# Norm sums as columns of tokens, in a two-layer decoder trunk

## The chip, the cores and the metric

The kernel runs on one core of one Trainium2 chip. The time is the device time of one execution in microseconds. All arithmetic is float32, or float32r: numbers are split into a high and a low part, and three float32r products stand for one float32 product.

## The reference

A trunk of two layers over 1024 tokens with 1024 features. Layer 0 is an mLSTM mixer and an MLP; layer 1 is latent attention with a shared key and value path and an MLP. What matters here are the norms over features, which stand ahead of and behind every mixer and MLP, and on three latents:

```python
def rmsnorm(x, g):
    xf = x.astype(jnp.float32)
    y = xf * lax.rsqrt(jnp.mean(xf * xf, axis=-1, keepdims=True) + EPS)
    return (y * g.astype(jnp.float32)).astype(x.dtype)

x = x + g1[:, None, :] * rmsnorm(y, norm_g[l, 1])        # after a mixer
h = modulate(rmsnorm(x, norm_g[l, 2]), sh2, sc2)         # ahead of the MLP
y = sqrelu_mlp(h, mlp_w1[l], mlp_w2[l])
x = x + g2[:, None, :] * rmsnorm(y, norm_g[l, 3])
# in mla_shared_kv and mla_mixer: rmsnorm of h's input, of c_kv (256 wide) and of cq (384 wide)
```

## The kernel before

Activations stand with features on the 128 partitions and tokens along the free axis: a block is 128 features by 512 tokens, and eight blocks make one half of the tokens. The two halves are worked on as two streams that overlap. While the one half goes through the dense products of an MLP, the other half's norms, residuals, latent projections and attention are put between them.

A norm over features is then a sum over partitions and over blocks. `square_to` (L501) squares each block on ACT and adds the squares on DVE (L507) into one 128x512 tile. `sums_rstd` (L509) gets the sum over partitions with one float32 product, whose stationary operand is a 128x128 matrix of ones (L511): every partition then holds the sums of all 512 tokens. What follows runs on 128x512 tiles: mean plus EPS on DVE (L513), and `rsqrt_` (L474), which is Ln and Exp on ACT (L476, L477) and one Newton step of three DVE instructions (L478, L479, L480). The result, `rstd`, is a 128x512 tile that later instructions multiply with. `rstd_steps` (L493) does both as a generator: squares, a pause, then the sums and the chain. Only PE's products move a number across partitions here.

There are 16 such sums in the program, called below by their number in order of time: 1 and 2 (first half) and 3 and 4 (second half) belong to layer 0's `residual` (L964) and `post` (L2776); 5 to the first half's `residual` in `to_x` (L2880); 6, 7 and 8 to its `latent` (L1694: the norm of the input, of c_kv, of cq); 9 and 10 to `post_second` (L2834); 11 to the second half's `to_x`; 12, 13 and 14 to its `latent`; 15 and 16 to its `post`.

`two_streams` (L2924) sets the order on PE from there on. The generator `other` yields numbers; each number is how many steps of the dense generator are put on PE before `other` goes on. The code adds the number to what is due, takes 1 (or 0.5 for a step that is part of a group) for each dense step, and stops when nothing is due; a 0 clears what is due. Every step's PE instructions are tied behind the step before. A dense step is mostly 12 or 24 products of 128x512. On each engine the instructions run in the order in which the scheduler put them; `tc.high_priority` moves an instruction ahead in that order.

Other lines that are spoken of: L299 to L301 are the three float32r products of `mm3`; L255 is the DVE evacuation of an MLP product; L246 and L247 split weights; L520 and L521 split an activation; L549 is `along_tokens`, which spreads a 128x4 tile along tokens with four products, and L2475 makes columns of sums with four products, both at the program's start; L1722 and L1723 are the products of the third latent projection.

Of the kernel before, what the change touches and what calls it, by code (L numbers as in the profile page):

```python
# [14 lines left out]
ALU = mybir.AluOpType  # L15
AX = mybir.AxisListType

P = 128
# [64 lines left out]
def kernel(  # L83
# [54 lines left out]
    def tmc(dt=F32):  # L138
        return sb.tile([P, 512], dt, tag="tmc", bufs=TMC, name=f"tmc_{next(uid)}")
# [4 lines left out]
    def small(n, dt=F32):  # L144
        return sb.tile([P, n], dt, tag=f"sm{n}", bufs=6, name=f"sm_{next(uid)}")
# [4 lines left out]
    def pc():  # L150
        return pp.tile([P, 512], F32, tag="pc", bufs=2, name=f"pc_{next(uid)}")
# [322 lines left out]
    def rsqrt_(y, v, t):  # L474

        nc.scalar.activation(t, v, AF.Ln)  # L476
        nc.scalar.activation(y, t, AF.Exp, scale=-0.5)  # L477
        nc.vector.tensor_mul(t, y, y)  # L478
        nc.vector.scalar_tensor_tensor(t, t, -0.5, v, ALU.mult, ALU.mult)  # L479
        nc.vector.scalar_tensor_tensor(y, t, 1.5, y, ALU.add, ALU.mult)  # L480

    def last_of(g):

        while True:
            try:
                next(g)
            except StopIteration as e:
                return e.value
# [4 lines left out]
    def rstd_steps(blocks, n):  # L493

        accs = []
        for b in blocks:
            square_to(accs, b)
        yield
        return sums_rstd(accs[0], n, tmc())

    def square_to(accs, b):  # L501
        q = tmc()
# [3 lines left out]
        else:  # L506
            nc.vector.tensor_add(accs[0], accs[0], q)  # L507

    def sums_rstd(acc, n, y):  # L509
        pt = pc()  # L510
        nc.tensor.matmul(pt, ones, acc, start=True, stop=True)  # L511
        v, t = tmc(), acc
        nc.vector.tensor_scalar(v, pt, 1.0 / n, EPS, ALU.mult, ALU.add)  # L513
        rsqrt_(y, v, t)
        return y

    def split_mod(hi, lo, u, sh):

# [445 lines left out]
    def residual(y, half, B, src, first, each=None, n3=1, n7=1):  # L964

        blk = src(half)
        yield 0
        rs = rstd_steps([y[k] for k in range(KD)], D)
        next(rs)
        yield first  # L970
        rstd = last_of(rs)
        yield 0
        for k in range(KD):
            with paced():
                nc.vector.scalar_tensor_tensor(
                    y[k], y[k], B[:, k : k + 1], rstd, ALU.mult, ALU.mult
                )
                nc.vector.tensor_add(y[k], y[k], blk(k))
                if each:
                    each(k)  # L980
            nc.sync.dma_start(xs_blk(k, half), y[k])
            if k % 4 == 3:
                yield n7 if k == KD - 1 else n3


    NPR = DFF // P // 2
# [707 lines left out]
    def latent(hf, behind):  # L1694

        ready = []

        def load(b):  # L1700
            with tc.high_priority(PRIO):
                w = []
                for i in range(1 if b == 2 else 2):
                    t = raw(F32R) if i else None
                    if i == 0:
                        t = sb.tile([P, 1024], F32R, tag="ws", bufs=WS, name=f"lw_{next(uid)}")
                    nc.sync.dma_start(t.bitcast(F32), lw[b, i])
                    w.append(t.rearrange("p (a b) -> p a b", b=P))
                ready.append(w)

        load(0)
        load(1)
        yield 0
        h = hf.xn

        def proj(b):
            if b < 4:
                load(b + 2)
            w, pt = ready.pop(0), pc() if b == 2 else ps()
            for k in range(KD):  # L1720
                if b == 2:
                    nc.tensor.matmul(pt, w[0][:, k], h.lo[k], start=k == 0, stop=False)  # L1722
                    nc.tensor.matmul(pt, w[0][:, k], h.hi[k], start=False, stop=k == KD - 1)  # L1723
                else:
                    mm3(pt, w[0][:, k], w[1][:, k], h.hi[k], h.lo[k], k == 0, k == KD - 1)
            return pt

        lb = lambda b: lbias[:, b : b + 1]
        hf.cs = hdv()
        for i in range(2):  # L1730
            nc.sync.dma_start(hf.cs[:, i], rope_d[i][:, ts(hf.i, H)])
        if hf.i:
            low = [
                sb.tile([P, n], F32R, tag=t, bufs=1, name=f"kk_{t}")[:, :H]
                for t, n in (("tma", 512), ("v7", 4 * VE))
            ]
            hf.kk = [hd(F32R), low]
            nc.sync.dma_start(hf.kk[0][:, 0:H].bitcast(F32), kkd[0])
            nc.sync.dma_start(low[0].bitcast(F32), kkd[1])
        else:  # L1740
            t = hdv(F32R)
            hf.kk = [t[:, 0], t[:, 1]]
        s = ts(hf.i, H)
        ck, cq0, cq1 = k4v(), k4v(), k4v()
        cq = [cq0[:, 0], cq0[:, 1], cq1[:, 0]]
        def scaled(o, m):

            pt = proj(m)
            if m < 2:

                evac(o, pt)
                pt = o

            if not rx:
                rx.append(sums_rstd(hf.xx, D, Cst.rearrange("p a b -> p (a b)")[:, :H]))
            nc.vector.tensor_mul(o, pt, rx[0])
            return o

        def based(o, m):
            nc.scalar.activation(o, scaled(o, m), AF.Identity, bias=lb(m))  # L1760

        rx = []
        for m in range(2):
            based(ck[:, m], m)
        rp = rope_key(scaled(tmc(), 2), hf, lb(2))
        next(rp)
        yield 0
        rs = rstd_steps([ck[:, 0], ck[:, 1]], 256)
        next(rs)
        based(cq[0], 3)  # L1770
        yield 0
        kr = last_of(rp)
        rstd_k = last_of(rs)
        nc.scalar.copy(hf.kk[0][:, s], kr)
        low = hf.kk[1][1] if hf.i else hf.kk[1][:, s]
        nc.vector.tensor_sub(low, kr, hf.kk[0][:, s].bitcast(F32))
        if not hf.i:
            for i in range(2):
                nc.sync.dma_start(kkd[i], hf.kk[i].bitcast(F32))
        for m in range(1, 3):  # L1780
            based(cq[m], 3 + m)
        yield 0
        behind()
        rs = rstd_steps(cq, 384)
        next(rs)
        hi, lo = k4v(F32R), k4v(F32R)
        with paced():
            for m in range(2):
                u = ck[:, m]
                nc.vector.scalar_tensor_tensor(u, u, col(KVL + m, 1), rstd_k, ALU.mult, ALU.mult)  # L1790
                split_mod(hi[:, m], lo[:, m], u, None)
        hf.ckv = ([hi[:, m] for m in range(2)], [lo[:, m] for m in range(2)])
        yield (2, 1.5)[hf.i]
        rstd = last_of(rs)
        yield 0
        if not hf.i:
            behind()
        ah, al, b = k4v(F32R), k4v(F32R), k4v(F32R)
        his, los = [ah[:, 0], ah[:, 1], b[:, 0]], [al[:, 0], al[:, 1], b[:, 1]]
        for m in range(3):  # L1800
            u = cq[m]
            nc.vector.scalar_tensor_tensor(u, u, col(QL + m, 1), rstd, ALU.mult, ALU.mult)
            split_mod(his[m], los[m], u, None)
        hf.cq = (his, los)
        yield 1 if hf.i else 1.5
# [970 lines left out]
    def post(hf, y, B, src, A, sh, m, waits):  # L2776
# [3 lines left out]
        def kept():  # L2780
            u = [hdv() for _ in range(4)]
            for b in range(4):
                nc.sync.dma_start(
                    u[b], m.keep[2 * b * P : (2 * b + 2) * P].rearrange("(k p) n -> p k n", p=P)
                )
            return FH(tiles=u)

        if hf.i:
# [3 lines left out]
            for k in range(4):  # L2792
                for j in (k, 4 + k):
                    nc.scalar.activation(y[j], y[j], AF.Identity, scale=A[:, j : j + 1])
                nc.vector.tensor_sub(d[k], y[4 + k], y[k])
        yield waits[3]
        if hf.i and m.rows:
            u = kept()
        rstd = last_of(rs)
        yield 0  # L2800
        if not hf.i:
# [32 lines left out]
    def post_second(hf, y, B, src, A, sh, wino=False):  # L2834
        yield from residual(y, hf.i, B, src, (2, 2)[hf.i], None, *((2, 3), (1, 1))[hf.i])
        rs = rstd_steps([y[k] for k in range(KD)], D)
        next(rs)
        yield (5, 5)[hf.i]
        rstd = last_of(rs)
        yield 0  # L2840
        if not wino:
            hf.h2 = Split()
            yield from normed(hf.h2, y, rstd, A, sh, ms[1].keep)
            return
        h = hf.h2 = Blocks()
        for k in range(KD):
            with paced():
                nc.vector.scalar_tensor_tensor(
                    y[k], y[k], A[:, k : k + 1], rstd, ALU.mult, ALU.mult
                )  # L2850
                nc.scalar.activation(y[k], y[k], AF.Identity, bias=sh[:, k : k + 1])
                if k % 2:
                    h.plain(y, k // 2)
            if k % 4 == 3:
                yield 1
        h.sums(y)
# [269 lines left out]
```

## Time and profile before

| | us |
|---|---|
| median of 3 runs | 2269.22 (2268.82 to 2272.16) |
| the profiled execution | 2272.61 |
| its span in the profile | 2270.8 |
| PE busy | 2238.3 (99%), 11050 instructions |
| DVE busy | 1669.0 (73%), 2717 instructions |
| ACT busy | 1113.0 (49%), 1937 instructions |
| granted TensorE clock | 0.997 |

Times of instructions are microseconds from the start of the span. A row of the timeline holds start, duration, engine, source line, operation, written and read tiles, shapes and a count. Matmuls overlap, so a matmul's duration is longer than the time after which the next one starts; what a product takes of PE is read from start to start. In rows of groups the number after the bar is the busy time, then the mean nanoseconds of one, then the idle time of the engine ahead of them. `tmc`, `tmp` and `hd` are 128x512 work tiles, `sm` is a 128x4 tile, and `pc`, `ps` and `pm` are tiles in PSUM.

### The profile page before, as it was taken

How to read it: one execution, taken by the hardware profiler on the slowest of the kernel's cores; microseconds unless marked ns; L12 is line 12 of the kernel's file. 1: busy time of each engine (PE TensorE's matmuls, PEld its weight loads, DVE VectorE, ACT ScalarE, POOL GpSimd, SP SyncE). 2: the span in 40 equal slices, each digit the busy share in tenths (PEclk: the TensorE clock that was granted, in tenths of full speed). 3: DMA queues.
4: the chain of work that ended last, by engine and by line, in shares of the span. 5: the costliest groups of instructions: out<-in, count | busy, mean ns of one | idle time of the engine just before them, and what ended most of it. 6: DMA issues, size and time to landing. Idle time of an engine off the chain costs nothing.

```text
span 2270.8 us, 30938 instructions
## 1 busy us (share of the span) xinstructions
PE 2238.3 (99%) x11050; PEld 1852.5 (82%) x11050; DVE 1669.0 (73%) x2717; ACT 1113.0 (49%) x1937; POOL 137.8 (6%) x238
## 2 busy tenths in 40 slices
PE   8999999999999999999999999999999999999998
PEld 6888888888887887778888877888888888888887
DVE  6677777889887787677774787777758967675556
ACT  4455434765434445544455555545545433464343
POOL 1000000001122220000000000000010111100000
PEclk9999999999999999999999999999999999999999
DMA  9544455667999888567687764874487777665431
GB/s 313 186 135 123 148 166 150 194 213 267 323 282 310 280 285 297 178 216 221 208 269 224 262 226 146 285 281 177 156 259 275 240 248 222 234 220 187 149 101 57
DMA packets 404651, 494.60 MB, mean 218 GB/s; under 512 B 29236, under 2 KB 270961, under 8 KB 404497
## 3 DMA queue, kind: packets, MB, share of 16 engines
q1 hardware_dynamic: 384320, 421.74, 57.7%
q0 software_dynamic: 20176, 70.89, 8.6%
q8 instruction: 87, 1.43, 0.3%
q14 instruction: 68, 0.55, 0.1%
HBM read 366.19 MB, written 126.35 MB: 217 GB/s over the span
## 4 chain that ended last, share of the span: by engine, by line
PE 82%; DVE 6%; DMA 5%; issue 4%; ACT 3%; POOL 0%; SPq 0%; DVEq 0%; ACTq 0%; POOLq 0%
PE ps L299 13%; PE ps L300 13%; PE ps L301 13%; PE pm L300 9%; PE pm L301 9%; PE pm L299 9%; DMA raw<-in_mlp_w_dram 2%; PE pc L299 2%; PE pc L301 2%; PE pc L300 2%; DVE wl L247 1%; PE pc L2113 1%; DMA raw<-s 1%; DVE k L255 1%; DMA lw<-wh 1%
## 5 line engine op out<-in xcount | busy, mean ns | idle before, releaser
L246 ACT CAST wh<-raw 128x1024 fp32r<-128x1024 f32 (+4 forms) x295 | 298.6, 1014 | 399.0 <-PE ps L300 140.4
L247 DVE TENSOR_TENSOR wl<-raw,wh 128x1024 fp32r<-128x1024 f32 (+4 forms) x295 | 347.8, 1181 | 173.9 <-ACT wh L246 147.0
L299 PE MATMUL ps<-k,wh 128*128 128x512 f32 x1109 | 438.9, 396 | 2.7 <-DVE k L521 1.2
L301 PE MATMUL ps<-k,wl 128*128 128x512 f32 x1109 | 432.6, 390 | 0.0
L300 PE MATMUL ps<-k,wh 128*128 128x512 f32 x1109 | 432.1, 390 | 0.0
L299 PEld LDWEIGHTS ps<-k,wh 128*128 128x128 f32 x1109 | 208.3, 188 | 50.1 <-issue 3.2
L301 PEld LDWEIGHTS ps<-k,wl 128*128 128x128 f32 x1109 | 208.2, 188 | 44.1
L300 PEld LDWEIGHTS ps<-k,wh 128*128 128x128 f32 x1109 | 208.4, 188 | 42.9 <-issue 1.4
L299 PE MATMUL pm<-wh,hd 128*128 128x512 f32 x488 | 191.6, 393 | 0.0
L301 PE MATMUL pm<-wh,hd 128*128 128x512 f32 x488 | 190.0, 389 | 0.0
L300 PE MATMUL pm<-wl,hd 128*128 128x512 f32 x488 | 189.9, 389 | 0.0
L255 DVE TENSOR_TENSOR k<-k,pm 128x512 f32<-128x512 f32 (+1 forms) x170 | 141.1, 858 | 63.7 <-PE pm L301 63.6
L300 PEld LDWEIGHTS pm<-wl,hd 128*128 128x128 f32 x488 | 91.7, 188 | 19.3 <-issue 0.5
L301 PEld LDWEIGHTS pm<-wh,hd 128*128 128x128 f32 x488 | 91.6, 188 | 19.1
L299 PEld LDWEIGHTS pm<-wh,hd 128*128 128x128 f32 x488 | 91.6, 188 | 19.1 <-issue 0.5
L299 PE MATMUL pm<-hd,wk 128*128 128x512 f32 x256 | 101.5, 396 | 2.0 <-ACT hd L520 2.0
L300 PE MATMUL pm<-hd,wk 128*128 128x512 f32 x256 | 100.2, 391 | 0.4 <-DVE hd L521 0.4
L301 PE MATMUL pm<-hd,wk 128*128 128x512 f32 x256 | 100.0, 391 | 0.0
L300 PE MATMUL pm<-hd,wh 128*128 128x512 f32 x256 | 99.6, 390 | 0.2 <-DVE hd L521 0.2
L299 PE MATMUL pm<-hd,wh 128*128 128x512 f32 x256 | 99.3, 390 | 0.5 <-ACT hd L520 0.5
L301 PE MATMUL pm<-hd,wl 128*128 128x512 f32 x256 | 99.6, 389 | 0.0
L1007 ACT ACTIVATE tmp<-tmp 128x512 f32<-128x512 f32 x80 | 50.4, 630 | 80.1 <-DVE tmp L255 71.0
(510 smaller groups left out, 4750.7 us busy)
## 6 DMA issues: line engine op xcount, KB each, us to landing
raw<-in_mlp_w_dram SPq DMA_DIRECT2D x158, 512.0 KB, 4.9
raw<-in_mlp_w_dram SPq DMA_DIRECT2D x128, 256.0 KB, 4.7
raw<-in_ada_w_dram SPq DMA_DIRECT2D x54, 512.0 KB, 4.7
raw<-in_a_w_in_dram SPq DMA_DIRECT2D x44, 512.0 KB, 4.0
lo<-wl POOLq DMA_DIRECT2D x32, 512.0 KB, 6.1
u<-k POOLq DMA_DIRECT2D x32, 512.0 KB, 5.2
raw<-s SPq DMA_DIRECT2D x32, 512.0 KB, 4.3
wk<-lo SPq DMA_DIRECT2D x64, 256.0 KB, 4.4
```

The costliest lines, as they stand in the source:

```text
L246: nc.scalar.copy(hi[:, :n], r[:, :n])
L247: i = nc.vector.tensor_sub(lo[:, :n], r[:, :n], hi[:, :n].bitcast(F32))
L255: return f(*a, **k)
L299: nc.tensor.matmul(o, lh, rh, start=start, stop=False)
L300: nc.tensor.matmul(o, lh, rl, start=False, stop=False)
L301: pe_last[0] = nc.tensor.matmul(o, ll, rh, start=False, stop=stop)
L1007: nc.scalar.activation(s, s, AF.Relu)
L2113: nc.tensor.transpose(pt[:, ts(m, P)], u.prs[i][kb // 4][:, ts(kb % 4, P)], ident)
```

## The change

The sums are made the other way round. For each of four groups of 128 tokens, the tile of summed squares is the stationary operand and one column of ones the moving one: four products give a 128x4 tile, in which a partition is a token and a column a group of tokens. L513's instruction and `rsqrt_` then work on 128x4, with high priority. A second generator step, `along_blocks`, spreads the result: four products, each with one column of the 128x4 tile broadcast as stationary operand and the identity as moving one, write 128x512 in PSUM, and ACT copies this to an SBUF tile. Between the two steps a pause of 0.5 is put at most places, and the pauses beside it are made shorter by as much.

```diff
@@ rstd_steps, sums_rstd
-        return sums_rstd(accs[0], n, tmc())
+        y = sums_rstd(accs[0], n)
+        yield
+        return along_blocks(tmc(), y)
...
-    def sums_rstd(acc, n, y):
+    def sums_rstd(acc, n):
+
+        pt = pc()[:, :4]
+        for t in range(4):
+            nc.tensor.matmul(
+                pt[:, t : t + 1], acc[:, ts(t, P)], ones[:, 0:1], start=True, stop=True
+            )
+        y, v, w = small(4), small(4), small(4)
+        with tc.high_priority(PRIO):
+            nc.vector.tensor_scalar(v, pt, 1.0 / n, EPS, ALU.mult, ALU.add)
+            rsqrt_(y, v, w)
+        return y
+
+    def along_blocks(dst, y):
+
         pt = pc()
-        nc.tensor.matmul(pt, ones, acc, start=True, stop=True)
-        v, t = tmc(), acc
-        nc.vector.tensor_scalar(v, pt, 1.0 / n, EPS, ALU.mult, ALU.add)
-        rsqrt_(y, v, t)
-        return y
+        for t in range(4):
+            nc.tensor.matmul(
+                pt[:, ts(t, P)], y[:, t : t + 1].to_broadcast([P, P]), ident, start=True, stop=True
+            )
+        evac(dst, pt)
+        return dst
@@ residual
         yield first
+        next(rs)
+        yield 0.5
         rstd = last_of(rs)
...
-                yield n7 if k == KD - 1 else n3
+                yield n7 if k == KD - 1 else max(n3 - 0.5, 0.5)
@@ latent
-            pt = proj(m)
-            if m < 2:
-
-                evac(o, pt)
-                pt = o
-
-            if not rx:
-                rx.append(sums_rstd(hf.xx, D, Cst.rearrange("p a b -> p (a b)")[:, :H]))
-            nc.vector.tensor_mul(o, pt, rx[0])
+            pt = o if m < 2 else proj(m)
+            nc.vector.tensor_mul(o, pt, rx)
             return o
...
-        rx = []
+        evac(ck[:, 0], proj(0))
+        rx = sums_rstd(hf.xx, D)
+        evac(ck[:, 1], proj(1))
+        rx = along_blocks(Cst.rearrange("p a b -> p (a b)")[:, :H], rx)
...
-        rstd_k = last_of(rs)
+        next(rs)
...
             based(cq[m], 3 + m)
+        rstd_k = last_of(rs)
...
-        yield (2, 1.5)[hf.i]
+        yield (1.5, 1)[hf.i]
+        next(rs)
+        yield 0.5
         rstd = last_of(rs)
@@ post
-        yield waits[3]
+        yield waits[3] - 0.5
         if hf.i and m.rows:
             u = kept()
+        next(rs)
+        yield 0.5
         rstd = last_of(rs)
@@ post_second
-        yield (5, 5)[hf.i]
+        yield 4.5
+        next(rs)
+        yield 0.5
         rstd = last_of(rs)
```

In the changed program the sums are L515, their mean plus EPS L520, and the spreading products L528; `rsqrt_` keeps its lines. On PE, the place of sum 6 before: the two projections into `ps` end, the sum follows, and then the third projection.

```order
L300 MATMUL ps_8344<-k_1397_7971,lw_7960 128x512
L301 MATMUL ps_8344<-k_1396_7970,raw_7962 128x512
L511 MATMUL pc_8329<-tmc_8131,ones 128x512
L1722 MATMUL pc_8377<-k_1391_7965,lw_8301 128x512
L1723 MATMUL pc_8377<-k_1390_7964,lw_8301 128x512
```

And with the change (L1741 and L1742 are the third projection):

```order
L300 MATMUL ps_8438<-k_1409_8015,lw_8004 128x512
L301 MATMUL ps_8438<-k_1408_8014,raw_8006 128x512
L515 MATMUL pc_8420<-ones,tmc_8220 128x1 x4
L528 MATMUL pc_8464<-ident,sm_8425 128x128 x4
L1741 MATMUL pc_8479<-k_1403_8009,lw_8392 128x512
L1742 MATMUL pc_8479<-k_1402_8008,lw_8392 128x512
```

The second projection, which the code puts between the two steps, has ended ahead of both, and the spreading products stand right behind the sums. At sum 12 four products of the second projection stand between them:

```order
L515 MATMUL pc_12741<-ones,tmc_12539 128x1 x4
L301 MATMUL ps_12759<-k_2237_12363,raw_12355 128x512
L299 MATMUL ps_12759<-k_2237_12363,lw_12353 128x512
L300 MATMUL ps_12759<-k_2238_12364,lw_12353 128x512
L301 MATMUL ps_12759<-k_2237_12363,raw_12355 128x512
L528 MATMUL pc_12785<-ident,sm_12746 128x128 x4
```

At sum 16 nothing stands between them on PE, since three dense steps take the 2.5 that are due there and the 0.5 behind it only makes up for the half that was too much:

```order
L301 MATMUL pm_16456<-wh_16383,hd_16161 128x512
L515 MATMUL pc_16491<-ones,tmc_16338 128x1 x4
L528 MATMUL pc_16506<-ident,sm_16496 128x128 x4
L299 MATMUL ps_16532<-k_2205_12185,wh_16416 128x512
```

On DVE the small chain stands there behind the two evacuations of that `pm` tile (L255), and the first use of the norm (L2830) behind it:

```order
L255 TENSOR_TENSOR k_2223_12341<-k_2223_12341,pm_16456 128x512
L255 TENSOR_TENSOR k_2224_12342<-k_2224_12342,pm_16456 128x512
L520 TENSOR_SCALAR sm_16497<-pc_16491 128x4
L478 TENSOR_TENSOR sm_16498<-sm_16496 128x4
L479 SCALAR_TENSOR_TENSOR sm_16498<-sm_16498,sm_16497 128x4
L480 SCALAR_TENSOR_TENSOR sm_16496<-sm_16498,sm_16496 128x4
L2830 TENSOR_TENSOR k_3052_16361<-k_3052_16361,tmc_16505 128x512 x2
```

At the other 13 sums the products between the sums and the spreading are 12 (sums 8, 11 and 15), 21 (sums 7 and 13), 24 (3, 5, 10, 14), 24 and four transposes (9), 27 (4), 37 (2) and 53 (1).

## The prediction

> **What bounds the kernel now.** I read the page first, then who PE waits for, then the stretches behind the sums, then the products one by one.
>
> ```profile
> span 2270.8 us, 30938 instructions
> PE 2238.3 (99%) x11050; PEld 1852.5 (82%) x11050; DVE 1669.0 (73%) x2717; ACT 1113.0 (49%) x1937; POOL 137.8 (6%) x238
> ```
>
> PE is busy for all but 32.5 us of the span; DVE and ACT have slack on average. Who PE waited for between 390 us (ahead of sum 1) and the last product, longest first; columns are total, times, longest:
>
> ```profile
> PE pc L2027 <- DVE sm L385: 2.7, 2, 2.2
> ...
> PE ps L300 <- DVE k L521: 1.1, 1, 1.1
> PE ps L299 <- DVE tmp L255: 1.1, 1, 1.1
> ...
> PE pc L511 <- DVE tmc L507: 0.5, 1, 0.5
> ...
> PE ps L299 <- ACT k L520: 0.4, 1, 0.4
> ...
> PE pc L2041 <- DVE k L521: 0.2, 1, 0.2
> ```
>
> These 13 rows add up to 14.7 us. That is all that lighter work on DVE and ACT could win back behind 390 us. Busy time by stretch, in the order PE, PEld, DVE, ACT, POOL, behind sum 2 and from sum 11 to sum 12:
>
> ```profile
> 445.00:461.00 16.00, 16.00 (x71) 12.87 (x70) 15.45 (x22) 15.12 (x24) 0.00 (x0) 1.00 0.85 267
> 1340.00:1375.00 35.00, 31.71 (x129) 23.58 (x129) 30.39 (x46) 22.16 (x38) 1.62 (x3) 1.00 0.64 218
> ```
>
> Behind sum 2 DVE works 15.45 of 16 us and PE does not pause once: the dense products cover the chain. The second stretch is the one of this kind where PE does wait (3.3 us of 35). The four rows with 1.1, 1.1, 0.5 and 0.4 above fall into it, 3.1 us together. So time here is PE's work plus a few waits, and an edit is judged first by what it adds to PE.
>
> **The change on PE.** What the sum costs today is read from start to start:
>
> ```profile
> 444.63 0.39 PE L299 MATMUL pm<-k,wh 128*128 128x512 f32 x1
> 444.86 0.39 PE L300 MATMUL pm<-k,wh 128*128 128x512 f32 x1
> 445.08 1.02 PE L511 MATMUL pc<-tmc,ones 128*128 128x512 f32 x2
> ...
> 446.17 0.39 PE L299 MATMUL ps<-k,wh 128*128 128x512 f32 x1
> ```
>
> A dense product takes 0.227 us (444.63 to 445.08 holds two). From 445.08 to 446.17 are the sum and one dense product: 1.09 - 0.23 = 0.86 us for the sum. The float32 product stands as two records.
>
> The new column products have a twin at the program's start: four float32 products with 128x1 results, also eight records.
>
> ```profile
> 43.83 0.95 PE L2475 MATMUL pc<-ones,tmp 128*128 128x1 f32 x8
> 44.63 0.48 PE L299 MATMUL ps<-k,wh 128*128 128x512 f32 x1
> 44.95 0.39 PE L300 MATMUL ps<-k,wh 128*128 128x512 f32 x1
> ```
>
> From 43.83 to 44.95 less one dense product is 0.89 us: 0.11 us a record, though each moves one column. Bounds: 0.80 (to the next start) and 0.95 (the row's duration). The row is of the same form with the same neighbours, so I take 0.89. One column thus costs as much PE as the 512 did.
>
> By the Trainium skill ("TensorE: Matmul & The Clock Gate", Back-to-back issue gap) a product with 1 to 64 columns takes about 60 cycles, or 25 ns; eight records would be 0.20 us and the forecast below about 11 us lower. The trace disagrees with 112 ns a record. The same page's section on LDWEIGHTS gives 107 ns for 128 weight columns, which is what the row looks like: the weights are what is paid.
>
> For the spreading, the nearest rows are the four products of L549 (eight records) and, among dense products, L383's four transposes (one record each):
>
> ```profile
> 14.45 1.06 PE L549 MATMUL ps<-ident,sm 128*128 128x128 f32 x8
> 15.35 0.27 PE L347 MATMUL ps<-ident,raw 128*128 128x128 f32 x1
> 556.88 0.60 PE L383 MATMUL pc<-ident,tma 128*128 128x128 f32 x4
> ...
> 557.54 0.39 PE L300 MATMUL ps<-k,wh 128*128 128x512 f32 x1
> ```
>
> L549 takes 0.90 from start to start. L383's four records take 0.66 - 0.23 = 0.43, so eight take 0.87. I take 0.87, bounds 0.87 and 0.90. A sum then costs PE 0.89 + 0.87 - 0.86 = **0.90 us more** (bounds 0.81 to 0.99). Nothing hides it, since PE has no pause there.
>
> **The change on DVE and ACT.** The first two rows are groups of today's chain; the next two are ACT's and DVE's kind of work on 128x4 (duration as least, median, most); the last two are the first and last instruction of one such small chain.
>
> ```profile
> L513 DVE TENSOR_SCALAR tmc<-pc 128x512 f32<-128x512 f32 x16 | 11.0, 687 | 9.3 <-PE pc L511 9.2
> L477 ACT ACTIVATE tmc<-tmc 128x512 f32<-128x512 f32 x14 | 8.8, 632 | 0.3
> L476 ACT ACTIVATE sm<-sm x18: 188/206/208, 11.5 to 373.7; 128x4 f32<-128x4 f32 x18
> L478 DVE TENSOR_TENSOR sm<-sm x18: 153/162/166, 12.0 to 374.5; 128x4 f32<-128x4 f32 x18
> 11.34 0.16 DVE L556 TENSOR_SCALAR sm<-sm 128x4 f32<-128x4 f32 x1
> 12.40 0.16 DVE L480 SCALAR_TENSOR_TENSOR sm<-sm,sm 128x4 f32<-128x4 f32 x1
> ```
>
> Four DVE instructions fall from 0.69 to 0.16 us: 2.1 us less DVE a sum, 34 us in all. As PE's waits show, hardly any of it was waited for. ACT trades two instructions of 0.63 for two of 0.21 and a copy of a 128x512 PSUM tile (0.57, row below), about even. The small chain takes 12.56 - 11.34 = 1.22 us from end to end when nothing is ahead of it.
>
> The change also adds a wait: the spreading products stand in PE's queue and need the chain's result, and all dense products behind them wait with them. With 24 products between, cover is 24 x 0.227 = 5.4 us against 1.2 us of chain and some queueing: no wait at 1 to 5, 7, 9, 10, 13 and 14. With 12 between (8, 15) cover is 2.7 us; I take nothing, bound 1 us each. That leaves 6, 16, 11 and 12.
>
> Sum 6 has no cover: the chain's 1.22 us and a step from PE to DVE and back (1.22 less 4 x 0.16 and 2 x 0.20 leaves 0.18 for the chain's five steps, some 0.04 each), **1.3 us** (bounds 1.2 and 2.0, the latter with a 128x512 activation ahead of Ln).
>
> Sum 16 has none either, and its chain stands behind two evacuations. Before:
>
> ```profile
> 1740.62 1.02 PE L511 MATMUL pc<-tmc,ones 128*128 128x512 f32 x2
> 1740.82 1.28 DVE L255 TENSOR_TENSOR k<-k,pm 128x512 f32<-128x512 f32 x2 [1.45 <-PE pm L301]
> 1742.63 0.68 DVE L513 TENSOR_SCALAR tmc<-pc 128x512 f32<-128x512 f32 x1
> 1744.55 0.57 ACT L259 COPY tmp<-ps 128x512 f32<-128x512 f32 x1
> ```
>
> The sum began at 1740.62. With the evacuations in front, the chain begins 1.5 us after that and ends at 2.7 to 2.8; the column products end at 0.9. PE waits **1.9 us** (bounds 1.2 and 3).
>
> Sums 11 and 12 are where DVE is late already:
>
> ```profile
> 1340.74 1.02 PE L511 MATMUL pc<-tmc,ones 128*128 128x512 f32 x2
> 1342.59 0.69 DVE L255 TENSOR_TENSOR tmp<-tmp,ps 128x512 f32<-128x512 f32 x1 [3.41 <-DMA m<-tmp]
> 1343.19 0.69 DVE L513 TENSOR_SCALAR tmc<-pc 128x512 f32<-128x512 f32 x1
> 1347.72 0.69 DVE L480 SCALAR_TENSOR_TENSOR tmc<-tmc,tmc 128x512 f32<-128x512 f32 x1
> 1373.86 1.12 PE L511 MATMUL pc<-tmc,ones 128*128 128x512 f32 x2 [0.47 <-DVE tmc L507]
> ```
>
> Sum 11 began at 1340.74, its chain 2.45 later, and the norm was there at 7.7. The small chain begins at 2.45 too (same evacuation ahead), loses two activations on ACT (0.63 each), and ends near 4.9: 1.3 us behind the end of its cover at 3.6. Spreading and copy make it 6.45, so the norm comes 1.2 us earlier than before. Sum 12 came 25.4 us after the norm, for work that DVE still has; now at 31.9 after sum 11, and with columns (0.89), chain (1.27; cover 4 x 0.227 lies within it) and spreading (0.87) the next projection starts at 34.9. Before it was 33.12 + 0.86 = 34.0. Both sums together cost **0.9 us**; bounds -0.9 (all 3.1 us of waits go) and 3.5 (nothing is won back).
>
> **The sum.** 14 x 0.90 = 12.6; 6 adds 1.3, 16 adds 1.9, 11 with 12 adds 0.9: 16.7 us. The profiled execution took 2272.6 (its span and 1.8 around it), so 2289.3 on its scale; that execution lay 3.4 above the median, 2269.2, and on the median's scale the forecast is **2286 us**. By the bounds: 14 x 0.81 - 0.9 + 1.2 + 1.2 = 12.8, and 14 x 0.99 + 3.5 + 2 + 3 + 2 = 24.4: 2282 to 2294.
>
> **The rivals.**
>
> DVE's relief pays for it. DVE loses 34 us of work; if everything PE waited for behind 390 us went (14.7 us), 16 x 0.90 + 3.2 - 14.7 = +2.9, or 2272, no change. It decides from 13 us of waits removed. Against it: only 3.1 of the 14.7 lie near a sum, and L2027's 2.7 is a wait for an instruction that the change does not touch. 0.04.
>
> Columns cost what they move. The sum's 512 columns take 0.86 us, 1.7 ns each; four products of one column would then be hidden: 16.7 - 16 x 0.89 = +2.5, again 2272. Against it stands the row of L2475, 112 ns a record. 0.03. (The time by the Trainium skill's rule on small products, "TensorE: Matmul & The Clock Gate", Back-to-back issue gap, would be 2275.)
>
> The spreading waits nearly everywhere. The chain crosses from DVE to ACT and back, each in order; today's chain at sum 11 took to 7.7, where its four instructions of 0.69 and two of 0.63 are 4.0. If the other 12 sums lose 1 us each: 2298. Against it are 5.4 us of cover and the priority. 0.10.
>
> Order elsewhere shifts. Buffers of `tmc` and `pc` change hands otherwise, and single waits of 1 to 2 us come or go: some 5 us either way, mostly inside the bounds; 0.10 for an end outside of them. That the chain isn't small, or the dense work changes, is excluded by the instructions as built.
>
> **How the numbers follow.** The forecast gets 0.73, with 2282 to 2294 as its own range. The range for 8 in 10 reaches towards the first two rivals below and most of the way to the third above: 2277 to 2297. About 0.2% is what a measurement here tells from no change, 4.5 us: faster needs under 2264.7, which no named rival reaches, so 0.03 out of the 0.10; same 0.05, from the first two rivals; slower 0.92.
>
> **What would show it.** In the profile after: eight records of L515 from start to start in about 0.89 us, L528 in 0.87; 224 more PE records (16 x 14); DVE busy down by about 34 us and ACT within 5; PE waits behind L480 of 1 to 2 us at sums 6 and 16 and fewer waits for DVE between 11 and 12. I am wrong if the column products take under 0.4 us, if waits far from the sums vanish, or if L528 waits at sums with 24 products between.

## The result

The changed kernel takes 2305.28 us (median; 2301.41 to 2309.34), the kernel before beside it 2270.69 (2268.82 to 2273.53). The ratio is 1.0151, 95% interval 1.0128 to 1.0175: about 34.6 us slower. The forecast was 2286 us, range 2277 to 2297. The direction was right; the loss is twice the one forecast, and the time lies outside the range.

### The profile page after: what moved, and what is told of

The parts are those of the page before. It is cut to its first block, busy times and chain, and to the rows that moved or that the text cites. A ratio compares the mean times of both kernels' runs of the same rounds, so it can differ in the third digit from the quotient of the medians.

```text
span 2305.4 us, 31425 instructions
## 1 busy us (share of the span) xinstructions
PE 2260.2 (98%) x11274; PEld 1880.0 (82%) x11274; DVE 1637.6 (71%) x2717; ACT 1105.9 (48%) x1952; POOL 138.0 (6%) x238
## 4 chain that ended last, share of the span: by engine, by line
PE 79%; DVE 9%; DMA 6%; issue 3%; ACT 2%; POOL 1%; SPq 0%; DVEq 0%; ACTq 0%; POOLq 0%
PE ps L299 13%; PE ps L301 13%; PE ps L300 13%; PE pm L301 9%; PE pm L300 9%; PE pm L299 9%; DMA raw<-in_mlp_w_dram 3%; PE pc L299 1%; PE pc L300 1%; PE pc L301 1%; DVE wl L247 1%; DVE tma L411 1%; DVE k L255 1%; PE pc L2131 1%; DMA raw<-s 1%
## 5 line engine op out<-in xcount | busy, mean ns | idle before, releaser
L246 ACT CAST wh<-raw 128x1024 fp32r<-128x1024 f32 (+4 forms) x295 | 298.1, 1013 | 398.0 <-PE ps L300 157.6
L255 DVE TENSOR_TENSOR k<-k,pm 128x512 f32<-128x512 f32 (+1 forms) x170 | 140.9, 857 | 74.7 <-PE pm L301 74.5
```

The lines of the kernel that those rows point to most:

```text
L246: nc.scalar.copy(hi[:, :n], r[:, :n])
L255: return f(*a, **k)
```

## The profile after

The profiled execution took 2307.45 us. The head of its page:

```profile
span 2305.4 us, 31425 instructions
...
PE 2260.2 (98%) x11274; PEld 1880.0 (82%) x11274; DVE 1637.6 (71%) x2717; ACT 1105.9 (48%) x1952; POOL 138.0 (6%) x238
```

PE has the 224 more records that were forecast, DVE 31.4 us less work (34 forecast) and ACT 7.1 less (within 5 forecast). But PE is idle for 45.2 us of the span (2305.4 - 2260.2) where it was idle for 32.5: its busy time rose by 21.9 us and the span by 34.6.

The products themselves, in the timeline of PE at sum 2 (start, duration, engine, line, operation, tiles, shapes, count):

```profile
443.43 0.95 PE L515 MATMUL pc<-ones,tmc 128*128 128x1 f32 x8
444.23 0.49 PE L300 MATMUL ps<-k,wh 128*128 128x512 f32 x1
444.56 0.40 PE L301 MATMUL ps<-k,wl 128*128 128x512 f32 x1
...
452.76 1.05 PE L528 MATMUL pc<-ident,sm 128*128 128x128 f32 x8
453.57 0.48 PE L300 MATMUL ps<-k,wh 128*128 128x512 f32 x1
453.89 0.39 PE L301 MATMUL ps<-k,wl 128*128 128x512 f32 x1
```

From 443.43 to 444.56 and from 452.76 to 453.89 are 1.13 us each; less one dense product, 0.90 for the columns and 0.90 for the spreading. Over the 16 sums the medians are 0.905 and 0.897, and 0.859 for the old sum, so a sum costs PE 0.905 + 0.897 - 0.859 = 0.94 us more, and 16 cost 15.1. The rows bear out the prediction's side. By the rule on small products of the Trainium skill ("TensorE: Matmul & The Clock Gate", Back-to-back issue gap) an estimate for the columns is 0.20 us; the trace disagrees.

Who PE waited for between 390 us and the last product (total, times, longest), the longest rows:

```profile
PE ps L299 <- ACT wh L246: 3.6, 1, 3.6
PE pc L528 <- DVE sm L480: 3.5, 3, 1.8
PE pc L2131 <- DVE tmc L1931: 2.4, 7, 1.3
PE pm L299 <- ACT wh L246: 2.4, 1, 2.4
PE ps L299 <- ACT k L537: 2.2, 1, 2.2
PE pm L301 <- DVE wl L247: 2.0, 3, 1.0
PE pc L2059 <- DVE raw L1939: 2.0, 2, 1.2
```

All rows together are 26.7 us, 14.7 before: 12.0 more. Only the second row is the new wait behind the chain: 1.3 us at sum 6, 1.8 at sum 16 and 0.4 at sum 12. The rest, 8.5 us more, stands at products that the change does not touch.

Sum 6 in the timeline, all engines:

```profile
923.20 0.95 PE L515 MATMUL pc<-ones,tmc 128*128 128x1 f32 x8
...
924.18 0.16 DVE L520 TENSOR_SCALAR sm<-pc 128x4 f32<-128x4 f32 x1 [4.30 <-PE pc L515]
...
925.25 0.16 DVE L480 SCALAR_TENSOR_TENSOR sm<-sm,sm 128x4 f32<-128x4 f32 x1
...
925.46 1.16 PE L528 MATMUL pc<-ident,sm 128*128 128x128 f32 x8 [1.32 <-DVE sm L480]
```

The chain takes 1.23 us from end to end (924.18 to 925.41), as the program's start had shown, and PE waits 1.32 where 1.3 was forecast. What the forecast does not have comes next. Busy time and granted clock around sum 6 (the columns are PE, PEld, DVE, ACT, POOL, then the granted clock, the DMA share and GB/s):

```profile
922.00:926.00 4.00, 2.68 (x18) 2.36 (x18) 0.65 (x4) 1.58 (x4) 0.00 (x0) 1.00 0.74 254
926.00:930.00 4.00, 4.00 (x15) 3.26 (x14) 1.29 (x2) 1.92 (x3) 0.00 (x0) 0.59 0.59 205
930.00:934.00 4.00, 4.00 (x18) 3.23 (x17) 1.28 (x2) 1.97 (x4) 0.00 (x0) 0.98 0.00 0
```

Behind the wait the clock is 0.59 for four microseconds: in the records of the granted clock it is one stretch of 3.41 us at 0.5, and a dense product takes 0.427 us in it instead of 0.227. Such a stretch loses PE 1.7 us and does not show as a wait; where PE also waits inside a stretch, it loses less. Between 390 us and the last product before had two of them (6.8 us at half clock), after has seven (23.9 us; the two near 1387 adjoin). That is 17.1 us more at half clock, **8.5 us lost**. The mean granted clock fell from 0.997 to 0.993, which is the same thing: 0.4% of the span. The other executions bear it out: after's four have 0.993 to 0.995, and those of the kernel before beside the experiments 0.996 to 0.999, 0.998 on average.

So the profiled execution is told by three terms: 15.1 us of PE's work, 12.0 of waits and 8.5 of half clock, 35.6 in sum against 34.6 by the spans.

## The experiments

The theory after this: PE's work as measured, waits behind the chain where nothing covers it, half-clock stretches behind them, and waits elsewhere that come from the pauses. The rivals: the pauses alone do it; or the products cost more than they look.

**The pauses alone** (e1_pacing). The changed kernel's pauses and order, with the one product of ones in place.

```diff
-        y = sums_rstd(accs[0], n)
+        y = sums_rstd(accs[0], n, tmc())   # one product, 128x512 chain, as before
         yield
-        return along_blocks(tmc(), y)
+        return y
```

> The changed kernel with the old sums put back: one product with the matrix of ones, the chain on 128x512, nothing spread. The changed pauses and the new order in the latent stay. Column theory (the loss is the columns' own: 15 us of PE work, waits for the spreading, and the half clock that follows a wait): 2268 to 2274. Pacing theory (a third or more of the loss comes from where the dense steps now stand, since sum 6 comes 5.4 us of dense work later and the loads behind it with it): 2279 to 2290.

2274.89 us against 2270.61, ratio 1.0021 (1.0011 to 1.0030). The pauses cost some 4 to 5 us by themselves; by subtraction, the products and what hangs on them do the rest. The time lies between the two expectations, 0.9 above the first.

**The products alone** (e6_products). The kernel before, and behind each of its sums four column products and four spreading products whose result nobody reads.

```diff
         nc.tensor.matmul(pt, ones, acc, start=True, stop=True)
+        more = pc()
+        for t in range(4):   # columns
+            nc.tensor.matmul(more[:, t : t + 1], acc[:, ts(t, P)], ones[:, 0:1], ...)
+        for t in range(4):   # spreading, from a tile that is there already
+            nc.tensor.matmul(more[:, ts(t, P)], cond[:, t : t + 1].to_broadcast([P, P]), ident, ...)
```

> The kernel before with, behind each old sum, four products of one column and four of 128 columns that nobody reads. Nothing waits for them and no pause is changed. If PE's work adds up one to one, as the traces read it (0.91 + 0.90 us a sum, 16 sums): +29, 2299 to 2301. If PE had room that the traces don't show: under 2290. If later work has something to wait for that moves with it (fewer waits): 2293 to 2298.

2305.23 us against 2269.77, ratio 1.0151 (1.0137 to 1.0165): 35.5 us for 16 x (0.905 + 0.897) = 28.8 us of added work, and 4 us above what was expected. The work is paid in full, since nothing covers it. Its profile has 2.5 us more waits than before and 6.8 us more at half clock (3.4 lost), though no product waits for anything new. So here some waits and stretches came with a mere shift of PE's work against the other engines.

**The columns without cover** (e2_columns). The kernel before with its own pauses; the spreading stands right behind the sum.

```diff
-        return sums_rstd(accs[0], n, tmc())
+        return along_blocks(tmc(), sums_rstd(accs[0], n))   # both as in the change
```

> The kernel before with the column form alone: pauses as before, the spreading right behind the chain. Eleven spreading products have no cover. Column theory: 15 us of PE work, eleven waits of 1.3 to 2 us and up to 1.7 us of half clock behind each: 2302 to 2325, at or above the changed kernel's 2305. Pacing theory: the waits cost the same, but the changed kernel's stray waits for weights (about 12 us) are not there: 2295 to 2312.

2321.35 us, ratio 1.0235 (1.0216 to 1.0254). The first row of its waits:

```profile
PE pc L526 <- DVE sm L480: 20.3, 10, 3.2
```

Ten waits of 2.0 us on average, where eleven were expected. In the records of the granted clock five of them have a half-clock stretch within 1.3 us of their end, the other five (at 892, 923, 1329, 1404 and 1441 us) have none. Without its pause the change would cost 51 us, not 35; the pause does cover the chain.

**The columns at two sums alone** (e7_open). The kernel before, with columns and spreading right behind at sums 6 and 16 and nowhere else.

```diff
+        if open_:                      # sum 16; sum 6 likewise in `latent`
+            return along_blocks(tmc(), sums_columns(accs[0], n))
         return sums_rstd(accs[0], n, tmc())
```

> The kernel before with the column form at sums 6 and 16 alone, the spreading right behind the chain. PE work 1.9 and waits 1.5 and 2.0 as seen: +5.4, 2276, if a wait costs itself alone; with a window of half clock behind both (1.7 each) +8.8, 2279.

2277.99 us against 2269.77, ratio 1.0037 (1.0024 to 1.0050): 8.2 us for two sums. Its wait for the chain, and the stretches behind both sums:

```profile
PE pc L536 <- DVE sm L480: 3.6, 2, 2.3
```

```profile
912.00:916.00 4.00, 4.00 (x15) 3.42 (x16) 1.29 (x2) 1.74 (x3) 0.00 (x0) 0.57 0.84 315
...
1744.00:1748.00 4.00, 3.70 (x15) 3.12 (x16) 2.05 (x5) 0.59 (x1) 0.00 (x0) 0.66 0.00 0
```

2 x 0.94 of work, 3.6 of waits and two stretches of 1.7 are 8.9; without the half clock they would be 5.5. The prediction's prices for these two sums were right but for the clock. The two profiles alone do not show this, since before's has two stretches as well, near 710 and 1014 us, and e7_open's has none there. All executions together do: the mean granted clock is 0.9966 in e7_open's five and 0.998 in the nine of the kernel before beside them, which is 3.2 us of the span.

**Cover at sums 6, 12 and 16** (e3_cover). The changed kernel, with the third latent projection put between columns and spreading, and one step between them in `post` instead of half a step.

```diff
         rx = sums_rstd(hf.xx, D)
         evac(ck[:, 1], proj(1))
+        third = proj(2)
         rx = along_blocks(...)
...
-        yield waits[3] - 0.5
+        yield waits[3] - 1
         next(rs)
-        yield 0.5
+        yield 1
```

> The changed kernel with dense work between columns and spreading at the three sums that had none or little: the third projection at 6 and 12, one dense step more at 4 and 16. If a wait also costs the half clock behind it (1.7 us a window): 3.9 us of waits and two windows back, 2297 to 2300. If a wait costs only itself: 2301 to 2303. If the waits only move: 2305.

2298.91 us, ratio 1.0131 (1.0116 to 1.0147), 6.4 us less than the changed kernel. The intervals of the two ratios overlap, but this kernel's longest execution (2301.46) is about as long as the changed kernel's shortest (2301.41). The waits behind the chain are gone and so are the stretches behind sums 6 and 16 (3.5 + 3.4 = 6.9). The profile has also lost a stretch at 1002 us and one of the two at 1387, which this edit was not meant to touch.

**Dense steps as before** (e5_steps). The change takes pauses of 2 into 2 and 0.5. Since a step counts 1 and the 0 behind them clears what is left over, the two take three dense steps where the 2 took two, and sum 6 stands one dense step later. This kernel is e3_cover with whole steps in the first half's `to_x`.

```diff
-        yield first
+        yield first - 1 if even else first
         next(rs)
-        yield 0.5
+        yield 1 if even else 0.5
...
-                yield n7 if k == KD - 1 else max(n3 - 0.5, 0.5)
+                yield n7 if k == KD - 1 else n3 if even else max(n3 - 0.5, 0.5)
```

> The covered version (dense work between columns and spreading at 6, 12, 16) and also the dense steps around the first half's residual ahead of sum 6 counted as before: one step less ahead of the columns of sum 5, one between them and the spreading, and none added. Sums 6 to 8 then stand where they stood in the kernel before or half a step ahead of it. If the remaining 28 us over the kernel before are PE work (15.2) and, for the rest, loads that stand in another order because a dense step more was put ahead of sum 6: 2286 to 2290. If that rest belongs to the columns wherever the steps stand: 2296 to 2301.

2293.42 us against 2269.77, ratio 1.0106 (1.0090 to 1.0122): 5.5 us less again by the medians (the intervals overlap a little), yet 3 us above what was expected. PE still waited 3.2 us for `wh` near 850 us.

**That wait, first try: loads** (e10_queue). In after, four loads of `xs` stand at the head of SP's queue near 843 us and wait there, ahead of the weight loads. Here the same four go through POOL's queue; PE's order is the same.

```diff
-                nc.sync.dma_start(t[b], ...)       # in x_ahead, first half of `to_x` alone
+                nc.gpsimd.dma_start(t[b], ...)
```

> The kernel with cover and dense step counts (e5_steps), with the four loads of the residual's first half (`k<-xs`) issued from POOL's queue instead of SP's; PE's order is the same. Theory (these four, waiting at the head of SP's queue for 6.5 us, hold back the weight loads behind them, and PE waits some 3.2 us for `wh` at 850 us, with a half-clock stretch behind it): that wait and its stretch go, 3.2 + 1.7 = 4.9 us less than e5_steps, about 2288.5 beside a before of 2269.8; the weight loads (L1173, L1727) are issued earlier than at 851 us. Rival (DVE and ACT are late there by their own work, the loads only stand beside it): the wait stays, within 1.5 us of e5_steps' 2293.4.

2293.54 us, ratio 1.0102 (1.0088 to 1.0117): no difference, and the wait for `wh` is 3.2 us as in e5_steps. The theory of the loads falls.

**That wait, second try: the weight folding.** What ACT and DVE did there in after:

```profile
849.61 0.40 ACT L1691 ACTIVATE tmc<-tmc,mods 128x128 f32<-128x128 f32 x1 [1.78 <-DVE tma L1685]
850.09 1.89 DVE L1685 SCALAR_TENSOR_TENSOR tma<-tmc,ada,tma 128x128 f32<-128x128 f32 x5
850.47 0.79 ACT L1691 ACTIVATE tmc<-tmc,mods 128x128 f32<-128x128 f32 x2 [0.46 <-DVE tma L1685]
...
852.27 1.03 ACT L246 CAST wh<-raw 128x1024 fp32r<-128x1024 f32 x1
...
853.35 0.50 PE L299 MATMUL pm<-hd,wh 128*128 128x512 f32 x1 [2.37 <-ACT wh L246]
```

L1683 to L1694 are `latent_weights`, which folds scales into six blocks of weights. Its last block stands ahead of L246 on ACT, and ACT waits in it for DVE; PE waits for L246. In the kernel before the last block began earlier:

```profile
815.61 0.27 DVE L1664 TENSOR_SCALAR tma<-tmc,ada 128x128 f32<-128x128 f32 x1
```

In after it began at 845.53:

```profile
845.53 0.27 DVE L1683 TENSOR_SCALAR tma<-tmc,ada 128x128 f32<-128x128 f32 x1
```

In the order of PE all six blocks stand one block's spacing (27 us of dense work) later. The reason is in the code: ahead of the folding a loop runs the second half's `post` of layer 0, one pause per dense step, whatever number the pause has. The change adds two pauses there (sums 3 and 4), so two more dense steps pass before the folding starts, and each block then starts at about the place where the next one stood before. e11_loop takes two other pauses out in that loop, which puts all six blocks back where before had them.

```diff
         rstd = last_of(rs)
-        yield 0
+        if not single[0]:      # true only in that loop; in `residual` and `post`
+            yield 0
```

> The changed kernel, with two pauses taken out in the loop that runs the second half's `post` of layer 0 one pause per dense step, whatever number the pause has: the `yield 0` behind the spreading at sums 3 and 4. So that loop again ends after as many dense steps as before, and the folding of the latents' weights (`latent_weights`, six blocks) starts at the same place in the dense work as before; after the change it stood one block later, with a block at 846 to 853 us. Theory (this slip is what makes ACT and DVE late at 850 us): no folding between 840 and 860 us, the wait for `wh` there (2.4 us) and the half-clock stretch behind it (1.7 us lost) go; 4 us less than the changed kernel's 2305.3, about 2301. Rival (ACT and DVE are late there for the order around sum 5, whatever the folding): the wait stays or another of its size takes its place, within 1.5 us of 2305.3.

2302.28 us (2301.08 to 2304.43), ratio 1.0140 (1.0123 to 1.0157). The stretch at 850 us in after, and then in e11_loop:

```profile
850.00:854.00 4.00, 1.64 (x7) 0.78 (x5) 3.71 (x9) 3.54 (x9) 0.53 (x1) 1.00 0.83 216
854.00:858.00 4.00, 3.47 (x10) 2.68 (x10) 3.47 (x5) 3.68 (x6) 2.13 (x4) 0.63 0.98 373
```

```profile
850.00:854.00 4.00, 4.00 (x20) 3.30 (x19) 4.00 (x7) 3.89 (x6) 0.79 (x5) 1.00 0.46 91
854.00:858.00 4.00, 4.00 (x19) 3.17 (x17) 3.90 (x6) 0.00 (x0) 0.81 (x3) 1.00 1.02 333
```

The wait for `wh` and the half clock are gone from there, so the slip is their cause. But a wait of 2.1 us for another tile (`hd`, L537) now stands at 860 us, where after has none, and all waits together fell by 1.8 us only (26.7 to 24.9). Another stretch is gone though the edit does not touch its place: PE waits 1.8 us at sum 16 as in after, and the clock stays whole. In after, then in e11_loop:

```profile
1772.00:1776.00 4.00, 2.47 (x10) 2.40 (x11) 0.81 (x5) 0.80 (x3) 0.00 (x0) 0.65 0.12 44
```

```profile
1772.00:1776.00 4.00, 3.15 (x18) 2.79 (x19) 1.85 (x6) 0.70 (x2) 0.00 (x0) 1.00 0.05 15
```

The median fell by 3.0 us of the 4 expected, but the intervals of the two ratios overlap.

**Both, and the pauses without the slip** (e12_both, e13_again, e14_pacing_loop). The same edit on e5_steps (twice) and on e1_pacing.

> The kernel with cover and dense step counts (e5_steps, 2293.4), with the same two pauses taken out. Theory: the wait for `wh` at 850 us (3.2 us) and its half-clock stretch (1.7 us) go, about 2288.5; what is left above before is PE's 15.2 us and some 3.5 us of waits and half clock. Rival (another wait of that size comes): within 1.5 us of 2293.4.

> The same kernel as e12_both. Theory (the kernel has two ways to run, one with more half-clock stretches, and the shorter was the one profiled): times again from 2290 to 2299; in an execution at 2290 to 2292 two half-clock stretches, in one at 2296 to 2299 four or more, and waits of some 3 us more in sum. Rival (the long executions are chance of that job): median within 1.5 us of 2290.9.

> The old sums with the changed kernel's pauses and order (e1_pacing, 2274.9, 4.3 above before), with the two pauses taken out of the loop that counts them one by one. Theory (what the pacing costs by itself is the slip of the weight folding): the wait for `wh` at 840 us is gone and the time is within 1.5 us of before, about 2270. Rival (the pacing costs by its order elsewhere, at sum 6 and the latents): within 1.5 us of 2274.9.

e12_both took 2297.24 us (2290.94 to 2299.26), ratio 1.0115 (1.0098 to 1.0131); the same kernel again 2294.12 (2292.55 to 2299.73), ratio 1.0101 (1.0085 to 1.0117). Neither differs from e5_steps' 1.0106, though the wait at 850 us is gone in both traces. Why is seen by the two profiled executions, the shortest of the first series and the longest of the second:

```profile
span 2288.8 us, 31425 instructions
...
PE 2253.1 (98%) x11274; PEld 1872.9 (82%) x11274; DVE 1638.3 (72%) x2717; ACT 1106.0 (48%) x1952; POOL 138.6 (6%) x238
```

```profile
span 2297.6 us, 31425 instructions
...
PE 2257.8 (98%) x11274; PEld 1878.3 (82%) x11274; DVE 1638.8 (71%) x2717; ACT 1105.9 (48%) x1952; POOL 138.5 (6%) x238
```

The same instructions take 8.8 us longer. The second has five stretches' worth of half clock where the first has two (17.1 us against 6.8, so 5.1 lost), and 21.6 us of waits against 18.1: 8.6 in sum. Where, for one, in the second:

```profile
1140.00:1144.00 4.00, 2.17 (x17) 1.76 (x15) 2.16 (x3) 1.70 (x3) 0.00 (x0) 1.00 0.97 357
1144.00:1148.00 4.00, 2.89 (x14) 2.88 (x14) 3.76 (x8) 0.59 (x1) 0.00 (x0) 0.52 0.22 70
1148.00:1152.00 4.00, 4.00 (x24) 3.92 (x23) 2.40 (x8) 1.02 (x4) 0.00 (x0) 0.62 0.83 226
```

So a wait or a stretch may come or go from execution to execution, and one that an edit removes can be made up elsewhere. e14_pacing_loop took 2273.74 us against 2272.69, ratio 1.0012 (1.0003 to 1.0021), e1_pacing 1.0021: by the ratios about half of the pauses' 4 to 5 us is the slip. The interval overlaps e1_pacing's, so neither expectation is settled. Nor can the traces place this cost: the profiled executions of both, 2268.6 and 2269.0 us of span, are shorter than before's.

The three terms in each profiled execution, against before's, in us. PE's work is the start-to-start price; half clock counts half of the stretches' time. Before's profiled execution lay 3.4 us above its median, so single rows can be off by that much:

| | PE work | waits | half clock | sum | span above before |
|---|---|---|---|---|---|
| after | 15.1 | 12.0 | 8.5 | 35.6 | 34.6 |
| e2_columns | 15.1 | 19.7 | 8.5 | 43.3 | 41.9 |
| e3_cover | 15.1 | 7.1 | 1.7 | 23.9 | 24.8 |
| e5_steps | 15.1 | 4.9 | 1.7 | 21.7 | 20.4 |
| e11_loop | 15.1 | 10.2 | 5.1 | 30.4 | 31.8 |
| e12_both | 15.1 | 3.4 | 0.0 | 18.5 | 18.0 |
| e13_again | 15.1 | 6.9 | 5.1 | 27.1 | 26.8 |
| e6_products | 28.8 | 2.5 | 3.4 | 34.7 | 32.3 |
| e7_open | 1.9 | 2.1 | 0.0 | 4.0 | 5.4 |

**DVE's relief** (e4_prio). The kernel before, with high priority on the 128x512 chain.

```diff
+        with tc.high_priority(PRIO):
             nc.vector.tensor_scalar(v, pt, 1.0 / n, EPS, ALU.mult, ALU.add)
             rsqrt_(y, v, t)
```

> The kernel before with high priority on its 128x512 chain, nothing else. If the chain's place in DVE's order is what makes PE wait between sums 11 and 12 (3.1 us there): 2267 to 2269. If not: 2269 to 2273, no difference.

2271.32 us, ratio 1.0003 (0.9993 to 1.0013). In its profile the norm of sum 11 is there 6.1 us after the sum's start, where it was 7.7, and PE waits 2.2 us in that stretch for 3.1; the median shows no gain from it.

**A cheaper sum** (e8_split, e9_early). If PE's work is what counts, the sum itself should be made cheaper: the summed squares are split into two float32r tiles, and two float32r products (0.227 us each) replace the float32 product of 0.86. In e8_split the split stands at the sum, at all sums; in e9_early ahead of the pause, at the ten sums over 1024 features outside the latents.

```diff
+            hi, lo = tmc(F32R), tmc(F32R)
+            nc.scalar.copy(hi, acc)
+            nc.vector.tensor_sub(lo, acc, hi.bitcast(F32))
-        nc.tensor.matmul(pt, ones, acc, start=True, stop=True)
+        nc.tensor.matmul(pt, ones_r, hi, start=True, stop=False)
+        nc.tensor.matmul(pt, ones_r, lo, start=False, stop=True)
```

> The kernel before with the sum's one float32 product (0.86 us) made as two float32r products (0.23 each): the tile of squares is split on ACT and DVE, as all operands here are. PE loses 16 x 0.41 = 6.5 us of work; ACT gains 16 x 0.63 and DVE 16 x 0.69, and each norm comes 1.3 us later. If PE's work is what counts: 2263 to 2266. If the later norm makes PE wait as much: 2269 to 2273.

> The kernel before, with the split of the summed squares into two float32r tiles put ahead of the pause between squares and sum, and only at the ten sums over 1024 features; the six sums in the latents (6, 7, 8, 12, 13, 14) keep the float32 product. Theory (what the split lost before was PE's wait for it, and the sum's price is PE work): no wait for the split is left, each of the ten sums takes two products of 0.227 us where it took 0.86, so 10 x 0.41 = 4.1 us less than before beside it, about 2265.7; PE waits between 390 and 2330 us near 15 in sum. Rival (ACT's copy and DVE's subtraction are late whatever the place, or one more instruction on each delays the other blocks): waits rise by 3 to 5 us and a half-clock stretch or two of 3.4 us come with them, 2269 to 2275.

e8_split took 2278.58 us, ratio 1.0039 (1.0026 to 1.0051), above both expectations. PE waits for the split:

```profile
PE pc L516 <- ACT tmc L514: 4.6, 2, 3.4
...
PE pc L517 <- DVE tmc L515: 1.5, 2, 1.0
```

These waits of 6.1 us, 2.1 us more of others and 6.8 us more at half clock (3.4 lost) are more than the 6.5 us that PE's work was to win. e9_early took 2270.06 against 2269.72, ratio 1.0003 (0.9994 to 1.0012): the waits for the split are nearly gone, but the 4.1 us expected did not come. Its profiled execution has waits and half clock within 1 us of before's (15.3 and 6.8) and a span 3.2 us shorter, but before's profiled execution lay about as much above its median; the median over 11 runs is no shorter, and where the gain goes was not seen. No kernel tried here beats the one before.

## Why the prediction was half right

**PE's work: right in kind, a little small.** 0.90 us a sum were forecast and 0.94 measured, 15.1 us in all against 14.4. The columns take 0.905 (0.89 forecast, bounds 0.80 to 0.95) and the spreading 0.897 (0.87, bounds 0.87 to 0.90). e6_products shows that nothing hides it. "Columns cost only what they move" is refuted.

**Waits behind the chain: right.** 1.3 at sum 6 and 1.9 at sum 16 were forecast, 1.3 and 1.8 came; at sum 12, four products of cover left 0.4. At sums with 12 or more products between there is none.

**What failed first: the price of a wait.** The prediction priced a wait at its own length and had no term for the clock. In after a half-clock stretch follows at both open sums, 1.7 us each; e7_open has both by itself, and in e3_cover they are gone with the waits. The price is not a fixed one: e11_loop has the same wait at sum 16 at full clock, and in e2_columns five of ten waits have no stretch, so that both came in after was in part chance. Over the whole program the stretches cost 8.5 us, 3.4 of it at these two sums, and the sum had nothing for them. The Trainium skill describes such a clock ("TensorE: Matmul & The Clock Gate", "What's actually happening"): it falls to one half after an idle window of about 3.4 us and comes back after as long a busy one. The length of the stretches, 3.41 us, agrees; but PE waited only 1.3 and 1.8 us ahead of those at sums 6 and 16. The advice of the Trainium skill to leave no gaps above some 3 us ("TensorE: Matmul & The Clock Gate", "Why this matters for your kernels") is not enough here: these waits, and one of 2.4 us (853 us in after), had a stretch.

**What failed second: "no wait elsewhere".** The prediction took the waits far from the sums as unchanged, and gave "order elsewhere shifts" 0.10 and 5 us either way. They grew by 8.5 us. Part of it has a cause that could have been read from the code: a pause that is counted as one step whatever its number (the loop ahead of the folding, 2.4 us of wait and 1.7 of half clock in the trace, of which e11_loop has 2.1 again at another product), and 2 + 0.5 that takes three dense steps (e5_steps, 5.5 us by the medians). The rest comes and goes between executions; which edit brings it is open.

**What failed third: the credit at sums 11 and 12.** Both sums together were to cost 0.9 us, since a norm that comes earlier would win back the rest. Sum 11, the copy that gives its norm, and the first product behind sum 12's spreading in after:

```profile
1363.58 0.95 PE L515 MATMUL pc<-ones,tmc 128*128 128x1 f32 x8
...
1368.34 0.59 ACT L259 COPY tmc<-pc 128x512 f32<-128x512 f32 x1 [0.31 <-PE pc L528]
...
1401.76 0.47 PE L1741 MATMUL pc<-k,lw 128*128 128x512 f32 x1
```

The norm is there at 5.35 us (6.45 forecast, 7.7 before), so that part was better than forecast, and PE did not wait at sum 11. But that product starts at 38.2 us, where 34.9 was forecast and 34.0 stood before: a cost of 4.2 us, with the same 120 dense products in between. PE waited there, between 1365 and 1405 us:

```profile
PE ps L299 <- ACT k L537: 2.2, 1, 2.2
PE ps L299 <- DVE tmp L255: 1.2, 1, 1.2
PE pc L528 <- DVE sm L480: 0.4, 1, 0.4
```

That is 3.8 us against 3.1 before, with 6.8 us at half clock beside it. DVE is busy without a pause there:

```profile
1384.00:1388.00 4.00, 1.22 (x5) 0.44 (x3) 4.00 (x8) 1.72 (x4) 0.00 (x0) 0.94 0.99 390
1388.00:1392.00 4.00, 3.30 (x8) 2.62 (x9) 4.00 (x8) 3.94 (x8) 0.00 (x0) 0.50 0.96 268
```

The work behind the norm, not the norm, is late. DVE's 31.4 us of relief won nothing that can be seen, which also settles the rival that it pays for the change.

The rival nearest to the result, 2298, came closer for a wrong reason: it put 12 us of waits at the covered sums, and they have none. The prediction's 0.05 for no change is less than the 0.04 and 0.03 of the two rivals that end there, a slip of addition on which nothing rests.

## What to carry to other kernels

Where PE is the bound, count small products by their records, not by the columns moved: here four float32 products of one column cost as much as one of 512. Price a wait of PE in a dense stretch at its length and allow for a half-clock stretch behind it, here 1.3 us and up to 1.7 more. And when a change adds a step to a generator, look up every loop that counts its steps: the number that a pause carries may not be what that loop counts.

## What was not expected of the hardware

Between 390 us and the last product the half-clock stretches are all 3.41 us long or twice that, and they begin in or behind gaps in PE's dense products, such as 1.4 us (before, at 709 us) and 3.7 us (after, at 1202). But not every such gap has one: e11_loop waits 2.1 us at 860 us and 1.8 at sum 16 at full clock, and in attention of the kernel before (1500 to 1620 us) gaps of 4 us between 512-column products, filled with smaller ones, have none. What decides it was not found, and the same kernel had two stretches in one execution and five in another (e12_both, e13_again), which makes differences of a few microseconds between single executions.
